# Lower parts of 16 weight tiles by an adding DMA, three pairs of part buffers and two raw slots, in a hybrid attention and DeltaNet layer

## The chip, the cores and the metric

The kernel runs on one core of a Trainium2 chip. The metric is the device time of one execution in microseconds (us), the median of several runs. The engines are named as in the profile: PE is TensorE's matmul and PEld its weight load, DVE is VectorE, ACT is ScalarE, POOL is GpSimd, and SP is SyncE, which here only issues transfers. An engine works through its queue in order.

## What is computed

One layer of a diffusion backbone on 512 latent tokens and 256 context tokens of width 1024, all in float32. Cut to what matters here:

```
h  = rms_norm(x)*(1+sc1)+sh1 ;  hc = the same for the context      # modulation: silu(c) @ w_ada
aq, ak, av, dq, dk, dv, dz, da, db, ga, gd = split(h @ w_in)       # context: hc @ w_in
y_attn = windowed attention (8 query heads, 2 key heads, window 128, context keys, sink)
o_dl   = gated DeltaNet, both directions, chunks of 64, started from the context's states
y   = sigmoid(ga)*(y_attn @ w_br_attn) + sigmoid(gd)*(norm(o_dl)*silu(dz) @ w_br_dn)
x   = x + gt1*(y @ w_out)
out = x + gt2*(square(relu(modulated_norm(x) @ w_mlp1)) @ w_mlp2)
```

## The kernel before

**Products in three parts.** A float32 operand is split into an upper part, rounded to the matmul's short float32 format (`fp32r`), and a lower part, what the rounding left. A product is then three matmuls, added up in PSUM: upper weight with upper input, upper weight with lower input, lower weight with upper input (`mm3`, L302 to L304; the same in L981 for the gate tiles and L1027 for the attention branch's projection). The lower part of a weight tile is so needed by the third matmul of a tile.

**Weight tiles.** A tile is 128 output columns of a matrix, 128 x 8 x 128 elements (512 KB; 256 KB for the branch projections). `wload` (L246) brings one in: SP loads it into a raw slot (`wr`, `NWR` = 4 slots, L248), ScalarE copies it, rounded, into the upper part (`wh`, L253), and VectorE subtracts that from the raw tile into the lower part (`wl`, L254). There are `NWS` = 2 pairs of `wh` and `wl`; a few calls give buffers of their own instead. A raw slot is free after the subtraction, a pair after the tile's last matmul.

**Which tiles go through it, and in which order.** Three early tiles in the prologue, with buffers of their own (L257 to L263); 60 tiles from the list `wq` (L363 to L366), in order: two key tiles of the DeltaNet (numbers 0 and 1), the attention's key tile (2), its four query tiles (3 to 6), its value tile (7), the DeltaNet's four value tiles (8 to 11) and four query tiles (12 to 15), three gate tiles (16 to 18), the attention branch's projection (19 to 26), 17 more gate tiles (27 to 43), the DeltaNet branch's projection (44 to 51), and the output projection (52 to 59). Then the MLP: tiles of `w_mlp1` with buffers of their own and 32 tiles of `w_mlp2`. A tile from the list is taken by `wnext` (L370), which hands out the tile that was prepared last time and calls `wload` for the next one, so one tile is prepared ahead:

```python
    wq = [lambda a=a: wload(*a) for a in wq]
    wn = [wq.pop(0)()]
    def wnext():
        w = wn.pop()
        if wq:
            wn.append(wq.pop(0)())
        return w
```

**Stages.** The prologue computes the modulation of the first norm (loads of `w_ada`, L213) and the modulated inputs, and multiplies the three early tiles along. Then the order of the code is woven: `weave` takes turns between generators of steps. The attention's key and query tiles are woven with the DeltaNet's decay matrices (`mats`, with L751 to L777 on VectorE); the rest of them, the value tile, the DeltaNet's value tiles and the first scores with the inversion of the chunks' triangular matrices (`invert`, L810 and L811, many small VectorE operations); the DeltaNet's query tiles and three gate tiles with the attention's units (`scores`: L507 to L536; `outputs`: transposes L566, splits L190 and L191, products L555 and L556, L587). After that come the context's scan beside the branch projection and gate tiles, the latent scan beside gate tiles, the DeltaNet branch's projection, the output projection and the MLP, which multiplies by seven products instead of eight in most of it (`Pair`, L1430).

**The other modulation weights.** `late_mod` (L1041) computes the other four modulation vectors on VectorE from 32 loads of `wada2`, 16 of them beside the latent scan, the rest around the output projection and the first MLP tiles. Each load takes a raw slot of the same tag `wr` (L1044), and the product is written to a piece of the arena (L1046 and L1047).

**Memory and order.** Most buffers come from an arena of 167 units of 1 KB per partition, handed out round robin (`alloc`). The order on each engine's queue follows the code, except that the framework's planner lets an instruction pass one that it expects to be blocked; on SP about 60 of the 205 loads stand elsewhere than in the code.

Of the kernel before, what the change touches and what calls it, by code (L numbers as in the profile page):

```python
# [8 lines left out]
F32 = mybir.dt.float32  # L9
F32R = mybir.dt.float32r  # L10
BF16 = mybir.dt.bfloat16
AF = mybir.ActivationFunctionType
ALU = mybir.AluOpType
# [1 line left out]
PSUM = bass.MemoryType.PSUM  # L15

NU = 167
NWR, NWS = 4, 2
FILL = 144, 28, 36, (8, 7, 3)
INV = 2, 12, 18, 0  # L20
QTS = 7, 5, 4, 7, 3, 6, 10, 7
# [13 lines left out]
P = 128  # L35
D = 1024
KT = D // P
# [65 lines left out]
def tile_layer(ctx: ExitStack, tc: tile.TileContext, I: dict, out: bass.AP, dbg=None):  # L103
    nc = tc.nc
    V, A, G, PE = nc.vector, nc.scalar, nc.gpsimd, nc.tensor
# [4 lines left out]
    wp = ctx.enter_context(tc.tile_pool(name="wp", bufs=1))  # L110
# [6 lines left out]
    def nm(s):  # L117
        uid[0] += 1
        return f"{s}_{uid[0]}"
# [8 lines left out]
    alloc, bank = mem.get, lambda n=1: banks.get(n * 512)  # L128
# [10 lines left out]
    r32 = lambda ap: ap.bitcast(F32R)  # L139
# [103 lines left out]
        V.tensor_scalar(modS[:, kt, :], mp[:, 1, :], bada[:, kt:kt + 1], None, op0=ALU.add)  # L243
        mp_.free()

    def wload(src, n=KT, bufs=None):  # L246
        raw = wp.tile([P, KT, P], F32, tag="wr", bufs=NWR, name=nm("wr"))[:, :n]
        nc.sync.dma_start(out=raw, in_=src)  # L248
        if bufs:
            hi, lo = (b.ap.rearrange("p (k c) -> p k c", k=KT) for b in bufs)  # L250
        else:
            hi, lo = (wp.tile([P, KT, P], F32, tag=t, bufs=NWS, name=nm(t))[:, :n] for t in ("wh", "wl"))
        A.activation(r32(hi), raw, AF.Copy)  # L253
        V.tensor_tensor(r32(lo), raw, hi, op=ALU.subtract)  # L254
        return r32(hi), r32(lo)

    early, EARLY = [], {T_AB: 0, T_DK: 0, T_DK + 1: 0}  # L257
# [2 lines left out]
    def load_early():  # L260
        bb = alloc(1024), alloc(1024)
        ebufs.extend(bb)
        early.append((wload(I["win"][list(EARLY)[len(early)]], bufs=bb), bank(2)))  # L263
# [10 lines left out]
    for src, nt, n, r in ((xs_, 4, SEQ, rx), (cs_, 2, CTX, rc)):  # L274
# [9 lines left out]
        w = 512  # L284
# [32 lines left out]
    for kt in range(KT):  # L317
        t = alloc(768)
# [38 lines left out]
    for n in range(2):  # L357
# [5 lines left out]
    wq = [(I["win"][t], KT) for t in (T_DK + 2, T_DK + 3, T_AK, *range(T_AQ, T_AQ + 4), T_AV, *range(T_DV, T_DV + 4),  # L363
                                      *range(T_DQ, T_DQ + 4), *(t + i for t, i in gates[:ND1]))]
    wq += [(I["wbr"][0, ct], 4) for ct in range(8)] + [(I["win"][t + i], KT) for t, i in gates[ND1:]]
    wq += [(I["wbr"][1, ct], 4) for ct in range(8)] + [(I["wout"][ct], KT) for ct in range(8)]  # L366
    wq = [lambda a=a: wload(*a) for a in wq]
    wn = [wq.pop(0)()]

    def wnext():  # L370
        w = wn.pop()
        if wq:
            wn.append(wq.pop(0)())
        return w

    def in_tile_steps(ti, with_ctx):

        for (_, e), t in zip(early, EARLY):
            if t == ti:
                return e  # L380
        w = wnext()
        acc = bank(2 if with_ctx else 1)
        for k in range(KT):
            mm3(acc[:, :512], w, hx[k:k + 1], start=(k == 0), stop=(k == KT - 1), ks=[k])
            if with_ctx:
                mm3(acc[:, 512:768], w, hc[k:k + 1], start=(k == 0), stop=(k == KT - 1), ks=[k])
            if k < KT - 1:
                yield
        return acc
# [258 lines left out]
    t, t2 = alloc(TOK), alloc(TOK)  # L648
# [325 lines left out]
    def gate_tiles(todo):  # L974

        for kind, i in todo:
            w = wnext()
            acc = bank()
            for k in range(KT):
                for p, (x, y) in enumerate(((0, 0), (0, 1), (1, 0))):  # L980
                    PE.matmul(acc.ap, w[x][:, k, :], hx[k][y], start=(k == p == 0), stop=(k == KT - 1 and p == 2))  # L981
                    yield
            if kind == T_GA:
                g = alloc(SEQ)
                act(g.ap, acc.ap, AF.Tanh, scale=0.5)
                V.scalar_tensor_tensor(gat[i].ap, g.ap, 1.0, gat[i].ap, op0=ALU.add, op1=ALU.mult)
                g.free()
            else:
                t = alloc(SEQ, True)
                if kind == T_GD:  # L990
                    act(t.ap, acc.ap, AF.Tanh, scale=0.5)
                else:
                    silu2(t.ap, acc.ap)
                (gdt if kind == T_GD else szt).append(t)
            acc.free()
# [23 lines left out]
    def br_a():  # L1019

        for ct in range(8):
            gat.append(alloc(SEQ, True))
            w = wnext()
            pa = bank()
            for j in range(4):
                for p, (x, y) in enumerate(((0, 0), (0, 1), (1, 0))):
                    PE.matmul(pa.ap, w[x][:, j, :], r32(Q[y][:, :, j, :]), start=(j == p == 0), stop=(j == 3 and p == 2))  # L1027
                    yield
            A.activation(gat[ct].ap, pa.ap, AF.Copy)
            pa.free()  # L1030
        for b in Qb:
            b.free()
# [6 lines left out]
    modT = const.tile([P, 4, 8], F32, name="modT")  # L1039

    def late_mod(grp):  # L1041

        for j in range(8):
            wa = wp.tile([P, KT, P], F32, tag="wr", bufs=NWR, name=nm("wa")).rearrange("p k c -> p (k c)")  # L1044
            nc.sync.dma_start(out=wa, in_=I["wada2"][grp, j])
            t = alloc(1024)  # L1046
            V.scalar_tensor_tensor(t.ap, wa, 0.5, scr.ap, op0=ALU.mult, op1=ALU.mult, accum_out=modT[:, grp, j:j + 1])  # L1047
            t.free()
            if j == 7:
                V.tensor_tensor(modT[:, grp], modT[:, grp], bada[:, 16 + 8 * grp:24 + 8 * grp], op=ALU.add)  # L1050
            yield

    late = (x for grp in range(4) for x in late_mod(grp))
    late_n = [0]

# [129 lines left out]
    scr = alloc(1024, True)  # L1185
# [22 lines left out]
    for g in range(2):  # L1208
# [12 lines left out]
        for a in range(2):  # L1221
            lo, hi = quad(a, 0), quad(a, 1)
# [36 lines left out]
    for qq in range(2):  # L1259
# [3 lines left out]
        for a in range(2):  # L1263
            n = 2 * qq + a
            t = alloc(512)
            ct = lambda ap: ap.rearrange("p (c t) -> p c t", t=CH)
            V.scalar_tensor_tensor(ct(t.ap), pt.ap.rearrange("p (c a t) -> p c a t", a=2, t=CH)[:, :, a], gdnh, ct(szt[n].ap),
                                   op0=ALU.mult, op1=ALU.mult)
# [12 lines left out]
    for ct in range(8):  # L1281
        w = wnext()
# [32 lines left out]
    for ct in range(8 - NHALF):  # L1315
        w = wnext()
# [35 lines left out]
    def load_first():  # L1352
        for i in range(NHALF):
            bufs = [alloc(1024), alloc(1024)]
            first.append([bufs, wload(I["wm1"][i], bufs=bufs)])
# [152 lines left out]
    for hf in range(4):  # L1508
        act_, xs = [], []
        for f in range(0 if hf else FT):  # L1510
            if first:
                bufs, _, acc = first.pop(0)
            else:
                bufs = [alloc(1024), alloc(1024)]
                w = wload(I["wm1"][f], bufs=bufs)
# [161 lines left out]
```

## Time and profile before

| | |
|---|---|
| median of 3 runs | 927.6 us (925.4 to 929.88) |
| the profiled execution | 928.46 us, of which the span of instructions 926.7 us |
| PE busy | 897.7 us, 97% of the span |
| PEld busy | 748.8 us, 81% |
| DVE busy | 665.5 us, 72% |
| ACT busy | 482.4 us, 52% |
| POOL busy | 12.1 us, 1% |
| HBM read | 95.46 MB; DMA 107 GB/s in the mean |
| granted TensorE clock | 0.998 |

The profile is of one execution. Ends of matmuls are modelled, so a PE that is busy is not a PE at its best rate; the matmuls of a tile follow each other every 0.23 us, although each is shown for longer. A row of a group gives engine, operation, output and inputs, shapes and count, then busy time and the mean duration of one in ns, then the engine's idle time ahead of the group and what ended it. The chain is the work that ended last, followed back from the end. Times of rows are from the start of the span.

### The profile page before, as it was taken

The numbers are of one execution on the slowest core, as the hardware profiler recorded it, in microseconds if no ns is written. First come the engines' busy times: TensorE is split into PE (matmuls) and PEld (weight loads), VectorE is DVE, ScalarE is ACT, GpSimd is POOL, SyncE is SP. The second block draws the span as 40 slices with busy tenths as digits, with TensorE's granted clock in tenths as the row PEclk, the third lists the DMA queues.
The fourth block names the chain that finished last, engine by engine and source line by source line (L and its number), as shares of the span: only waits on it lengthen the run. The fifth ranks groups of instructions, "written<-read, shape, count | busy, mean of one in ns | idle before, by whom it ended". The sixth has DMA issues, their size and how long they took to land.

```text
span 926.7 us, 19276 instructions
## 1 busy us (share of the span) xinstructions
PE 897.7 (97%) x8228; PEld 748.8 (81%) x8228; DVE 665.5 (72%) x1116; ACT 482.4 (52%) x857; POOL 12.1 (1%) x26
## 2 busy tenths in 40 slices
PE   8999999989999999999999999999999999999998
PEld 6688677867777787878888888987898899889976
DVE  4666799996877997367866978995587377538632
ACT  5467654357567787475554434563355145425420
POOL 0000000000000002000000000000000000000000
PEclk9999999999999999999999999999999999999999
DMA  9911112110000132324524575543313341232021
GB/s 362 366 47 47 48 48 69 47 46 24 22 15 23 58 115 72 115 93 140 182 71 148 184 252 190 179 140 113 137 47 109 103 152 43 94 129 99 2 91 45
DMA packets 29605, 98.79 MB, mean 107 GB/s; under 512 B 3664, under 2 KB 4176, under 8 KB 29520
## 3 DMA queue, kind: packets, MB, share of 16 engines
q1 hardware_dynamic: 29520, 97.57, 30.8%
q8 instruction: 64, 1.05, 0.5%
q14 instruction: 21, 0.17, 0.1%
HBM read 95.46 MB, written 2.10 MB: 105 GB/s over the span
## 4 chain that ended last, share of the span: by engine, by line
PE 64%; DVE 19%; ACT 7%; DMA 6%; issue 3%; SPq 0%; DVEq 0%; ACTq 0%
PE banks L1430 11%; PE banks L302 10%; PE banks L303 10%; PE banks L304 10%; PE banks L981 9%; DVE wl L254 3%; DVE m L191 2%; DMA m<-in_wm 2%; PE banks L1027 2%; PE banks L1093 2%; DMA wa<-in_wada 2%; ACT m L154 1%; DVE m L811 1%; PE banks L566 1%; DVE m L810 1%
## 5 line engine op out<-in xcount | busy, mean ns | idle before, releaser
L304 PE MATMUL banks<-m,wl 128*128 128x512 f32 (+1 forms) x568 | 210.6, 373 | 3.5 <-DVE wl L254 3.5
L302 PE MATMUL banks<-m,wh 128*128 128x512 f32 (+1 forms) x568 | 213.0, 376 | 0.6 <-ACT wh L253 0.2
L303 PE MATMUL banks<-m,wh 128*128 128x512 f32 (+1 forms) x568 | 210.3, 370 | 0.0
L253 ACT ACTIVATE wh<-wr 128x1024 fp32r<-128x1024 f32 (+1 forms) x92 | 90.4, 984 | 131.7 <-PE banks L303 104.5
L1430 PE MATMUL banks<-m,m 128*128 128x256 f32 x1008 | 125.7, 286 | 3.3 <-DMA m<-in_wm 2.0
L1430 PEld LDWEIGHTS banks<-m,m 128*128 128x128 f32 x1008 | 123.8, 194 | 5.5 <-DMA m<-in_wm 2.2
L254 DVE TENSOR_TENSOR wl<-wr,wh 128x1024 fp32r<-128x1024 f32 (+1 forms) x92 | 103.9, 1129 | 33.5 <-ACT wh L253 31.1
L304 PEld LDWEIGHTS banks<-m,wl 128*128 128x128 f32 x568 | 106.5, 188 | 23.3 <-DVE wl L254 5.4
L302 PEld LDWEIGHTS banks<-m,wh 128*128 128x128 f32 x568 | 107.0, 188 | 20.0 <-ACT wh L253 1.3
L190 ACT ACTIVATE m<-m 128x512 fp32r<-128x512 f32 (+2 forms) x118 | 82.3, 720 | 77.8 <-DVE m L1288 12.6
L303 PEld LDWEIGHTS banks<-m,wh 128*128 128x128 f32 x568 | 107.0, 188 | 17.7 <-DVE m L191 0.3
L191 DVE TENSOR_TENSOR m<-m,m 128x512 fp32r<-128x512 f32 (+2 forms) x118 | 92.5, 806 | 21.9 <-ACT m L190 17.1
L981 PE MATMUL banks<-m,wh 128*128 128x512 f32 x320 | 104.0, 399 | 1.3 <-ACT m L154 1.1
L1557 DVE SCALAR_TENSOR_TENSOR m<-banks,modT,m 128x512 f32<-128x512 f32 x32 | 24.0, 750 | 80.3 <-PE banks L304 80.3
L981 PEld LDWEIGHTS banks<-m,wh 128*128 128x128 f32 x320 | 59.3, 188 | 13.6 <-ACT m L154 1.3
L981 PE MATMUL banks<-m,wl 128*128 128x512 f32 x160 | 65.2, 408 | 0.0
L302 PE MATMUL banks<-m,m 128*128 128x256 f32 (+1 forms) x136 | 44.7, 342 | 2.0 <-ACT m L308 1.2
L1047 DVE SCALAR_TENSOR_TENSOR m<-wa,m 128x1024 f32<-128x1024 f32 x32 | 39.0, 1220 | 9.9 <-DMA wa<-in_wada 9.7
L303 PE MATMUL banks<-m,m 128*128 128x256 f32 (+1 forms) x136 | 45.4, 341 | 0.0
L304 PE MATMUL banks<-m,m 128*128 128x256 f32 (+1 forms) x136 | 44.5, 337 | 0.1
L154 ACT ACTIVATE m<-banks,st 128x512 f32<-128x512 f32 (+1 forms) x32 | 23.5, 738 | 25.7 <-DVE st L523 25.5
L981 PEld LDWEIGHTS banks<-m,wl 128*128 128x128 f32 x160 | 30.0, 188 | 6.5
(254 smaller groups left out, 1352.7 us busy)
## 6 DMA issues: line engine op xcount, KB each, us to landing
wr<-in_wm SPq DMA_DIRECT2D x40, 512.0 KB, 3.9
wr<-in_win SPq DMA_DIRECT2D x39, 512.0 KB, 3.4
wa<-in_wada SPq DMA_DIRECT2D x32, 512.0 KB, 3.6
m<-in_wm SPq DMA_DIRECT2D x24, 512.0 KB, 3.3
m<-in_wada SPq DMA_DIRECT2D x16, 512.0 KB, 9.9
m<-in_xT SPq DMA_DIRECT2D x8, 512.0 KB, 5.1
wr<-in_wbr SPq DMA_DIRECT2D x16, 256.0 KB, 2.6
wr<-in_wout SPq DMA_DIRECT2D x8, 512.0 KB, 4.3
```

Source lines behind the costliest of these rows:

```text
L154: r = A.activation(out_, in_, func, **kw)
L190: A.activation(r32(hi), src, AF.Copy)
L191: (eng or V).tensor_tensor(r32(lo), src, hi, op=ALU.subtract)
L253: A.activation(r32(hi), raw, AF.Copy)
L254: V.tensor_tensor(r32(lo), raw, hi, op=ALU.subtract)
L302: PE.matmul(acc, w[0][:, k, :], xhi, start=(start and i == 0), stop=False)
L303: PE.matmul(acc, w[0][:, k, :], xlo, start=False, stop=False)
L304: PE.matmul(acc, w[1][:, k, :], xhi, start=False, stop=(stop and i == n - 1))
L981: PE.matmul(acc.ap, w[x][:, k, :], hx[k][y], start=(k == p == 0), stop=(k == KT - 1 and p == 2))
L1047: V.scalar_tensor_tensor(t.ap, wa, 0.5, scr.ap, op0=ALU.mult, op1=ALU.mult, accum_out=modT[:, grp, j:j + 1])
L1430: PE.matmul(dst, r32(self.w[w][i][:, k * P:(k + 1) * P]), xs7[x][k][j], start=(n == 0), stop=(n == 11))
L1557: V.scalar_tensor_tensor(xn_[ct], accs[ct].ap, modT[:, 3, ct:ct + 1], xn_[ct], op0=ALU.mult, op1=ALU.add)
```

## The change

For tiles 3 to 18 of the list, the lower part is no longer made by VectorE. ScalarE copies the upper part a second time, with a scale of -1, into the lower part's buffer, and POOL issues a transfer that reads the same weights from HBM again and adds them to what lies there: weight minus upper part. The raw slot is then needed by the upper part's copy only. All tiles of the list are prepared two ahead instead of one. There are three pairs of part buffers instead of two and two raw slots instead of four, which is the same memory. The loads of `late_mod` no longer use raw slots: each goes to the piece of the arena that held the product, and the product is written over it.

```diff
-NWR, NWS = 4, 2
+NWR, NWS = 2, 3
+WAHEAD = 2
+LODMA = 3, 19
...
-    def wload(src, n=KT, bufs=None):
+    def wload(src, n=KT, bufs=None, late=False):
+
         raw = wp.tile([P, KT, P], F32, tag="wr", bufs=NWR, name=nm("wr"))[:, :n]
         nc.sync.dma_start(out=raw, in_=src)
...
         A.activation(r32(hi), raw, AF.Copy)
-        V.tensor_tensor(r32(lo), raw, hi, op=ALU.subtract)
+        if late:
+            A.activation(r32(lo), hi, AF.Copy, scale=-1.0)
+            G.dma_start(out=r32(lo), in_=src, accum_op=ALU.add)
+        else:
+            V.tensor_tensor(r32(lo), raw, hi, op=ALU.subtract)
         return r32(hi), r32(lo)
...
-    wq = [lambda a=a: wload(*a) for a in wq]
-    wn = [wq.pop(0)()]
+    wq = [lambda a=a, i=i: wload(*a, late=LODMA[0] <= i < LODMA[1]) for i, a in enumerate(wq)]
+    wn = [wq.pop(0)() for _ in range(WAHEAD)]
 
     def wnext():
-        w = wn.pop()
+        w = wn.pop(0)
         if wq:
             wn.append(wq.pop(0)())
         return w
...
         for j in range(8):
-            wa = wp.tile([P, KT, P], F32, tag="wr", bufs=NWR, name=nm("wa")).rearrange("p k c -> p (k c)")
-            nc.sync.dma_start(out=wa, in_=I["wada2"][grp, j])
-            t = alloc(1024)
-            V.scalar_tensor_tensor(t.ap, wa, 0.5, scr.ap, op0=ALU.mult, op1=ALU.mult, accum_out=modT[:, grp, j:j + 1])
-            t.free()
+            wa = alloc(1024)
+            nc.sync.dma_start(out=wa.ap, in_=I["wada2"][grp, j])
+            V.scalar_tensor_tensor(wa.ap, wa.ap, 0.5, scr.ap, op0=ALU.mult, op1=ALU.mult, accum_out=modT[:, grp, j:j + 1])
+            wa.free()
```

## The prediction

> **What bounds the kernel now.** I read the page's busy line first, then the busy tenths by slice (23.2 us each), then the shares of the chain that ended last.
>
> ```profile
> PE 897.7 (97%) x8228; PEld 748.8 (81%) x8228; DVE 665.5 (72%) x1116; ACT 482.4 (52%) x857; POOL 12.1 (1%) x26
> PE   8999999989999999999999999999999999999998
> DVE  4666799996877997367866978995587377538632
> ACT  5467654357567787475554434563355145425420
> DMA  9911112110000132324524575543313341232021
> PE 64%; DVE 19%; ACT 7%; DMA 6%; issue 3%; SPq 0%; DVEq 0%; ACTq 0%
> ```
>
> TensorE looks busy everywhere, yet the chain gives VectorE 19% of the span, and the slices show where: VectorE stands at 9 tenths from slice 5 to slice 8, while ScalarE stands at 3 to 5 and the DMA engines at 1 to 2. That is the attention input, in which 16 weight tiles are consumed that the change treats differently. So I asked for the two stretches around the attention, for the group of the lower-part subtractions in the first, and for the chain there (start, duration, what).
>
> ```profile
> 96.00:206.00 110.00, 103.67 (x1245) 81.55 (x1244) 103.74 (x188) 54.41 (x95) 2.07 (x4) 1.00 0.16 54
> 206.00:304.00 98.00, 91.57 (x654) 72.86 (x652) 75.42 (x128) 65.76 (x122) 0.00 (x0) 1.00 0.07 20
> L254 DVE TENSOR_TENSOR wl<-wr,wh 128x1024 fp32r<-128x1024 f32 x10 | 12.2, 1224 | 0.0
> 99.78 1.14 DVE wl L254
> 194.43 1.13 DVE wl L254
> ```
>
> The columns of the first two rows are the stretch, then the busy time of PE, PEld, DVE, ACT and POOL, granted clock, DMA share and GB/s. From 96 to 206 us VectorE is busy 103.74 of 110.00 us: it sets the pace. Ten of the 16 subtractions lie there, all ten on the chain; the last two rows are the first and the last, each worth 1.14 us of the chain. From 206 to 304 us (attention proper, a chain of scores, maximum, exponentials, transposes) no engine is full: DVE 75.42 and ACT 65.76 of 98.00 us. What TensorE itself lost shows in its weight loads' waits, for 96 to 206 us (first three rows) and for 206 to 304 us (total us, times, longest):
>
> ```profile
> PEld banks L756 <- DVE m L755: 2.3, 3, 1.3
> PEld banks L737 <- DVE m L769: 2.1, 2, 1.7
> PEld banks L304 <- DVE wl L254: 1.6, 1, 1.6
> PEld banks L556 <- DVE m L191: 2.6, 5, 0.9
> PEld banks L566 <- DVE m L581: 1.9, 2, 1.6
> PEld banks L841 <- ACT m L833: 1.8, 1, 1.8
> PEld banks L981 <- ACT m L154: 1.3, 1, 1.3
> ```
>
> In the first stretch TensorE waits 2.3 + 2.1 + 1.6 = 6.0 us for VectorE, and 110.00 - 103.67 = 6.3 us without work at all. This is what a lighter VectorE can win there before TensorE is the bound. In the second it waits 2.6 + 1.9 = 4.5 us for VectorE and 1.8 + 1.3 = 3.1 us for ScalarE.
>
> **The change part by part.** The durations:
>
> ```profile
> L254 DVE TENSOR_TENSOR wl<-wr,wh 128x1024 fp32r<-128x1024 f32 x76 | 92.9, 1222 | 28.0 <-ACT wh L253 25.6
> L253 ACT ACTIVATE wh<-wr 128x1024 fp32r<-128x1024 f32 x76 | 80.4, 1059 | 120.9 <-PE banks L303 104.2 <-DMA wr<-in_wm 6.8 <-PE banks L981 5.1
> wr<-in_win SPq DMA_DIRECT2D x39, 512.0 KB, 3.4
> m<-in_wada SPq DMA_DIRECT2D x16, 512.0 KB, 9.9
> ```
>
> *Removed:* 16 VectorE subtractions, 16 x 1.22 = 19.6 us of busy time, or 16 x 1.14 = 18.2 us of pace. In the first stretch 10 x 1.14 = 11.4 us leave a path that VectorE sets, but TensorE follows only until its own waits are gone. Bounds: 0 (TensorE's waits stay, for other instructions) and -11.4. I take **-6.0**, the waits on VectorE above. In the second stretch VectorE loses about five (5.7 us of pace) against 4.5 us of waits on it; this goes together with the next part.
>
> *Added on ScalarE:* 16 copies with scale -1, at the 1.06 us of the upper part's copy of the same shape: 17.0 us. In the first stretch they lie beside 110.00 - 54.41 = 55.6 us of idle ScalarE. Queued behind each is the next ScalarE work, the exponentials and attention splits, and VectorE and TensorE wait for those. In the second stretch the bounds are -4.5 (VectorE's waits all go) and +5.3 (five copies of 1.06 all on the path); I take **-1.0**, since waits on VectorE (4.5) outweigh those on ScalarE (3.1) by 1.4.
>
> *Added on POOL and the DMA engines:* 16 adding transfers of 512 KB. POOL is busy 2.07 us in the first stretch (four memsets) and not at all in the second, so issuing hides; behind a waiting issue stand only those memsets, which the joining of the inverse's halves needs late. No row shows a transfer that adds. The nearest are a plain one, 3.4 us to landing, and the 9.9 us of loads behind a full queue. It must also read what it adds to, so I bound it by 3.4 us and by twice 9.9 = 19.8, and take twice 3.4 = 6.8, as the DMA engines are 0.16 and 0.07 busy here. Is there cover? Upper parts are copied once per tile, two tiles ahead after the change, when the third tile back has left its buffer. Today's copies, every second one of the tightest row of tiles:
>
> ```profile
> 135.11 1.05 ACT L253 ACTIVATE wh<-wr 128x1024 fp32r<-128x1024 f32 x1
> 152.12 1.06 ACT L253 ACTIVATE wh<-wr 128x1024 fp32r<-128x1024 f32 x1 [0.70 <-PE banks L303]
> 170.84 1.05 ACT L253 ACTIVATE wh<-wr 128x1024 fp32r<-128x1024 f32 x1
> 188.82 1.06 ACT L253 ACTIVATE wh<-wr 128x1024 fp32r<-128x1024 f32 x1
> ```
>
> Two tiles last 17.0, 18.7 and 18.0 us. After two ScalarE copies (2.1 us) 14.9 us are left for a transfer of 6.8. It costs **0**; without that cover, the excess over 14.9 us.
>
> *Moved: three pairs of part buffers, two tiles ahead.* Today a lower part can come so late that TensorE waits; the 1.6 us above is one case and is counted. In the branch and output projections (480 to 565 us) there is another:
>
> ```profile
> PEld banks L304 <- DVE wl L254: 2.2, 3, 1.3
> 538.06 3.99 DMA wa<-in_wada
> SPq L1045 <- DVE wl L254: 55.2, 13, 11.2
> ```
>
> A third pair lets VectorE run a tile further ahead, so these 2.2 us can go: bounds 0 and -2.2. The modulation weights also leave the raw slots for the arena. Today their issue waits 55.2 us in total for a subtraction that frees a slot, and such loads stand on the chain (the second row is one of 3.99 us); from the arena they can be issued earlier. Both point one way: I take **-2.2**.
>
> *Two raw slots instead of four.* First place, the prologue, whose loads run at the DMA engines' limit (slices 0 and 1 at 9 tenths):
>
> ```profile
> 13.21 0.33 SPq L248 DMA_DIRECT2D wr<-in_win  x1
> 14.41 13.72 SPq L213 DMA_DIRECT2D m<-in_wada  x10
> 19.21 1.22 DVE L254 TENSOR_TENSOR m<-wr,m 128x1024 fp32r<-128x1024 f32 x1
> 28.52 1.04 ACT L253 ACTIVATE m<-wr 128x1024 fp32r<-128x1024 f32 x1
> ```
>
> The third early weight is issued at 13.21. With two slots it needs the slot of the first, free at 19.21 + 1.22 = 20.43, so 7.2 us later. If the planner lets the modulation loads pass (it orders SP's queue by readiness), the load lands at about 20.4 + 9.9 = 30.3 instead of before the copy at 28.52: +1.8. If SP stays blocked, up to +7.2. I take **+1.8**. Second place, the DeltaNet branch projection, with its short tiles:
>
> ```profile
> 500.00:524.00 24.00, 24.00 (x108) 19.81 (x106) 17.86 (x28) 11.55 (x18) 0.00 (x0) 1.00 0.55 186
> 502.34 0.23 PE banks L303
> wr<-in_wbr SPq DMA_DIRECT2D x16, 256.0 KB, 2.6
> L253 ACT ACTIVATE wh<-wr 128x512 fp32r<-128x512 f32 x16 | 10.0, 627 | 10.9 <-PE banks L981 8.3 <-PE banks L1027 2.3 <-PE banks L303 0.3
> L254 DVE TENSOR_TENSOR wl<-wr,wh 128x512 fp32r<-128x512 f32 x16 | 11.0, 686 | 5.5 <-ACT wh L253 5.5
> ```
>
> TensorE has no gap here; a tile is 12 matmuls of 0.23 = 2.8 us. A raw slot cycles in 2.6 + 0.63 + 0.69 = 3.9 us for two tiles of 5.5, which leaves 1.6 us for queueing; four residual loads of 512 KB pass through as well. Bounds 0 and +5 (about one transfer and a copy late); I take **+0.5**. In the MLP a tile is twice as long with the same two slots: 0.
>
> *Sum:* -6.0 - 1.0 + 0 - 2.2 + 1.8 + 0.5 = -6.9. The profiled execution took 928.46 us (span 926.7), 0.9 above the median of 927.6, so 921.6 on its own time and 920.7 on the median: **921 us**.
>
> The Trainium skill has a rule that speaks against the change: "SBUF — State Buffer", Who interferes with whom, says that a transfer issued from GpSimd has its descriptors built through a port pair shared with VectorE, and starves while VectorE runs copies, casts or tensor_scalar in a two-port mode, though not under tensor_tensor. By that exception the sum stays; were every VectorE instruction to block, the transfers would be late as in the third rival. The groups that I saw on VectorE there are tensor_tensor, reductions and transposes; no run here yet shows a transfer issued from POOL.
>
> **The rivals.**
> *All of the relief arrives.* VectorE's path shortens by 11.4 in the first stretch, and its 4.5 us of waits go in the second: 928.5 - 11.4 - 4.5 - 2.2 + 2.3 = 912.7 on the profiled execution's time, **912 us** on the median. For it: all ten subtractions are on the chain. Against: TensorE has only 6.3 us without work.
> *Another engine takes the place.* ScalarE's copies, put between a finished product and the next step, delay what VectorE gets, and the 7.0 us of relief go: 928.5 - 2.2 + 2.3 = 928.6, with half of the relief 925.1; **927 us**. For it: the waits on ScalarE after 206 us. Against: its 55.6 idle us.
> *The lower parts come too late (the other side).* Place: TensorE's first matmul with the lower part, tiles between 120 and 206 us. It decides from 14.9 us per transfer. At 19.8 us (or if POOL's issue is held up as long) a tile needs (2.1 + 19.8)/2 = 11.0 us against today's (188.82 - 135.11)/6 = 9.0, so 2.0 us on each of eight tiles: +16, and the relief of 6.0 is not felt: 921 + 16 + 6 = 943, less what slack at either end absorbs: about **938 us**. For it: no transfer of the kind is in the trace. Against: the nearest row says 3.4.
> *Two raw slots bind.* SP blocked for 7.2 us in the prologue and +5 in the branch projection, instead of 2.3: 921 + 9.9 = **931 us**. Against: the planner's freedom on SP, and a slot cycle shorter than two tiles.
> That the change doesn't do what it says (lower parts still on VectorE) the diff excludes.
>
> **How the numbers follow.** Chances: forecast 0.46 (own range 913 to 926), all relief 0.12, another engine 0.20, late lower parts 0.14, raw slots 0.08. A difference of 0.5%, 4.6 us, is about what a measurement of this kernel can tell from no change: 923.0 to 932.2. Faster: 0.36 of the forecast's share, 0.12, and 0.02 of the third case: 0.50. Same: 0.10 of the forecast, 0.16, 0.02 of the slots' case: 0.28. Slower: the rest, 0.22. The range reaches below the all-relief case and up to the late transfers: 908 to 938.
>
> **What would show it.** Right: VectorE's busy time from 96 to 206 us falls by about 12 us and the stretch shortens by some 6; the two ScalarE copies stand side by side; transfers on a POOL queue land in 5 to 10 us; no TensorE wait for that queue. Wrong: weight loads of L304 released by a DMA into the lower part; ScalarE's waits in TensorE's list above 5 us; the first matmul after the prologue later by more than 2 us; waits for raw weights from 500 to 524 us.

## The result, and the profile after

The changed kernel takes **919.7 us** (median of 5 runs, 918.87 to 921.45) against 927.25 us (5 runs, 925.4 to 929.88) of the kernel before: ratio 0.9921, 95% interval 0.9898 to 0.9943. The profiled execution took 919.03 us, its span 917.3. The prediction was 921.0. The number is right; most of its terms are not.

The page after, its busy line, the shares of its chain, and two rows of its transfers (the last number is us from issue to landing):

```profile
PE 892.9 (97%) x8228; PEld 748.7 (82%) x8228; DVE 648.8 (71%) x1100; ACT 497.5 (54%) x873; POOL 26.0 (3%) x42
PE 81%; DVE 8%; ACT 7%; issue 2%; DMA 2%; SPq 0%; ACTq 0%; DVEq 0%
wl<-in_win POOLq DMA_DIRECT2D x16, 512.0 KB, 5.5
m<-in_wada SPq DMA_DIRECT2D x48, 512.0 KB, 5.0
```

VectorE's share of the chain fell from 19% to 8% and TensorE's rose from 64% to 81%. The adding transfer lands 5.5 us after its issue, near the 6.8 that were estimated. The same two stretches around the attention as in the prediction, and three short ones (stretch, busy time of PE, PEld, DVE, ACT and POOL, granted clock, DMA share, GB/s), after:

```profile
24.00:28.00 4.00, 3.42 (x22) 1.54 (x22) 3.95 (x8) 1.75 (x3) 0.00 (x0) 0.76 1.01 398
28.00:32.00 4.00, 4.00 (x27) 3.20 (x19) 1.99 (x7) 2.45 (x4) 0.00 (x0) 0.81 1.02 419
96.00:206.00 110.00, 103.32 (x1216) 82.31 (x1206) 94.71 (x178) 63.95 (x105) 10.69 (x14) 0.98 0.46 102
145.00:150.00 5.00, 4.60 (x14) 3.24 (x15) 4.90 (x12) 3.29 (x5) 0.86 (x1) 0.66 0.23 21
206.00:304.00 98.00, 93.69 (x760) 74.52 (x749) 71.52 (x126) 70.15 (x128) 3.46 (x4) 1.00 0.21 44
```

The short ones before:

```profile
24.00:28.00 4.00, 3.44 (x24) 1.62 (x25) 3.98 (x8) 1.92 (x4) 0.00 (x0) 1.00 1.04 424
28.00:32.00 4.00, 4.00 (x30) 3.11 (x29) 3.10 (x8) 2.80 (x5) 0.00 (x0) 1.00 1.02 416
145.00:150.00 5.00, 5.00 (x31) 4.39 (x30) 4.91 (x11) 1.08 (x2) 0.00 (x0) 1.00 0.31 105
```

From 96 to 206 us VectorE's busy time fell by 9.0 us (103.74 to 94.71), yet TensorE works no longer in the stretch than before (103.32 against 103.67). What its weight loads mainly wait for there now (total us, times, longest):

```profile
PEld banks L414 <- ACT m L411: 4.7, 5, 2.4
PEld banks L744 <- issue: 3.9, 5, 2.2
PEld banks L573 <- ACT m L156: 1.7, 2, 1.4
PEld banks L744 <- DVE m L784: 0.9, 2, 0.5
PEld banks L744 <- DVE m L783: 0.8, 1, 0.8
```

VectorE is named for 1.7 us instead of 6.0; ScalarE for 6.4, where its rows before came to 3.8 (L411 is the square in the attention's norm of queries and keys). The waits changed their name more than their sum.

To see where the time came from, the next table sets the starts of the same work in each profiled execution against the kernel before, in us (minus is earlier). The columns are the last matmul of list tiles 0, 12, 18 and 57 (before: 70.0, 203.5, 301.2 and 553.9 us), the first output of the MLP's second quarter (713.7) and the last output (922.9). The lower rows are the experiments of the next section. Each row is one execution. "Clock" gives where its granted clock fell to half for 3.4 us (us from the start; before: 860), which costs a row up to 1.7 us.

| | tile 0 | tile 12 | tile 18 | tile 57 | 2nd quarter | last | clock |
|---|---|---|---|---|---|---|---|
| the change | +1.1 | +1.7 | -0.6 | -0.8 | -5.0 | -9.5 | 26, 146 |
| without adding transfers | +1.5 | +2.4 | +2.7 | +2.5 | -1.4 | -4.6 | 25, 155 |
| arena loads alone | -0.1 | 0.0 | +0.3 | -0.1 | -0.3 | -2.8 | none |
| third pair, one ahead, no adding | +1.2 | +1.1 | +1.1 | +1.0 | -3.2 | -6.4 | 25, 209 |
| the change, one ahead | +1.3 | +1.5 | -0.8 | -0.9 | -5.1 | -10.6 | 25, 117 |
| no lower work at all | +0.4 | +0.7 | -2.1 | -1.4 | -5.6 | -10.6 | 144 |
| negation on VectorE | +0.6 | -0.6 | -0.9 | -1.0 | -5.3 | -6.3 | 250, 854 |
| "list with two pairs" | +1.6 | +1.6 | 0.0 | -0.1 | -4.4 | -8.9 | 26, 129 |
| two raw slots alone | +1.5 | +1.5 | +1.3 | +1.1 | +4.9 | +2.7 | 26, 593 (twice as long) |
| early raw weights in the pairs | -0.4 | 0.0 | -2.2 | -2.5 | -1.5 | -5.9 | 115, 569 |

The last column flatters most of them: from 780 us on, the profiled execution before had one wait of 2.0 us for an MLP load, which is 0.6 us or less in all rows but the second, the fourth and the negation on VectorE, and a drop of the granted clock, which of the others only the negation on VectorE had there:

```profile
PE banks L1430 <- DMA m<-in_wm: 2.0, 1, 2.0
```

```profile
860.00:890.00 30.00, 29.98 (x192) 27.51 (x191) 16.18 (x25) 13.47 (x16) 0.00 (x0) 0.95 0.01 2
```

So the column of the second quarter is the one to read.

Through the attention, where the prediction saw 7.0 of its 9.2 us of gains, the change moved the end of tile 18 by 0.6 us (from tile 0 on by 1.7 us, with a drop of the clock on the way). More than 4 us came between tile 57 and the MLP's second quarter, where the prediction saw nothing.

### The profile page after: what moved, and what is told of

Same layout as the page of the kernel before. It is cut to its first block, busy times and chain, and to the rows that moved or that the text cites. A ratio compares the mean times of both kernels' runs of the same rounds, so it can differ in the third digit from the quotient of the medians.

```text
span 917.3 us, 19321 instructions
## 1 busy us (share of the span) xinstructions
PE 892.9 (97%) x8228; PEld 748.7 (82%) x8228; DVE 648.8 (71%) x1100; ACT 497.5 (54%) x873; POOL 26.0 (3%) x42
## 4 chain that ended last, share of the span: by engine, by line
PE 81%; DVE 8%; ACT 7%; issue 2%; DMA 2%; SPq 0%; ACTq 0%; DVEq 0%
PE banks L309 14%; PE banks L310 14%; PE banks L311 14%; PE banks L988 11%; PE banks L1436 11%; PE banks L1034 2%; PE banks L1099 2%; ACT m L156 2%; PE banks L1111 1%; DMA m<-in_wm 1%; PE banks L1130 1%; PE banks L573 1%; DVE m L193 1%; PE banks L636 1%; PE banks L744 1%
## 5 line engine op out<-in xcount | busy, mean ns | idle before, releaser
L1436 PE MATMUL banks<-m,m 128*128 128x256 f32 x1008 | 123.6, 284 | 1.8 <-DVE m L193 1.0
L1436 PEld LDWEIGHTS banks<-m,m 128*128 128x128 f32 x1008 | 121.9, 192 | 3.6 <-DVE m L193 1.7
L192 ACT ACTIVATE m<-m 128x512 fp32r<-128x512 f32 (+2 forms) x118 | 82.5, 720 | 73.2 <-PE banks L1436 13.4
L261 DVE TENSOR_TENSOR wl<-wr,wh 128x1024 fp32r<-128x1024 f32 (+1 forms) x76 | 84.2, 1109 | 26.2 <-ACT wh L256 24.0
L1053 DVE SCALAR_TENSOR_TENSOR m<-m,m 128x1024 f32<-128x1024 f32 x32 | 38.9, 1219 | 12.3 <-DMA m<-in_wada 12.2
```

Source lines behind the costliest of these rows:

```text
L192: A.activation(r32(hi), src, AF.Copy)
L1053: V.scalar_tensor_tensor(wa.ap, wa.ap, 0.5, scr.ap, op0=ALU.mult, op1=ALU.mult, accum_out=modT[:, grp, j:j + 1])
L1436: PE.matmul(dst, r32(self.w[w][i][:, k * P:(k + 1) * P]), xs7[x][k][j], start=(n == 0), stop=(n == 11))
```

## The experiments

The first experiments take the change apart, the later ones test the reasons. Each ratio is to the kernel before, timed beside it; differences between experiments are given in us of the 927 us.

**Without the adding transfers.**

```diff
-LODMA = 3, 19
+LODMA = 0, 0
```

> The changed kernel with an empty list of adding transfers (LODMA = 0, 0): all lower parts are subtracted on VectorE again; three pairs of part buffers, two raw slots, two tiles ahead and the modulation weights in the arena stay. Theory of the buffers (the profile of after shows the attention stretch no shorter, and 7 of the 9 us won lie behind 500 us): 916 to 922 us. Theory of the prediction (the adding transfers win 6.0 us from 96 to 206 us and 1.0 behind it, the rest nets to 0): 926 to 928 us.

Measured: 923.49 us, ratio 0.9957 (0.9942 to 0.9973). It lies between the two: the buffers alone win 4 us, and the adding transfers another 3.3 us (0.9921 against 0.9957). By the table their share is there at tile 18: +2.7 without them, -0.6 with them, 3.3 us. Little of it comes before tile 12: from tile 0 to there, each with one drop of the clock, the run without them lost 0.9 us and the change 0.6.

**The adding transfers alone**, on the kernel before, with its four raw slots, two pairs and one tile ahead.

```diff
 NWR, NWS = 4, 2
+WAHEAD = 1
+LODMA = 3, 19
...
```

> The kernel before with the adding transfers for tiles 3 to 18 and nothing else: four raw slots, two pairs, one tile ahead, modulation weights in raw slots. Theory of the buffers: 925 to 930 us, as the negated copies on ScalarE eat what VectorE wins; with one tile ahead there are about 9 us a tile, less 2.1 for the two copies, against 5.5 to landing, so no long wait for lower parts. Theory of the prediction: 921 to 923 us.

Measured: 925.35 us, ratio 0.9978 (0.9963 to 0.9994): 2.0 us, not the 7.0 of the prediction's two terms. Here TensorE does wait for the new transfer, from 90 to 304 us:

```profile
PEld banks L311 <- DMA wl<-in_win: 3.0, 2, 2.1
```

No such row stands among the waits of the changed kernel from 96 to 304 us. With two pairs the transfer's 5.5 us are not always covered; with three they are.

**The modulation weights' loads into the arena alone.**

```diff
-            wa = wp.tile([P, KT, P], F32, tag="wr", bufs=NWR, name=nm("wa")).rearrange("p k c -> p (k c)")
+            wa = alloc(1024)
...
```

> The kernel before with the 32 modulation weights of late_mod loaded into the arena instead of raw slots, nothing else. If the loads that waited for a slot (55.2 us of SP's queue, transfers on the chain from 530 to 561 us) cost the path: 922 to 925 us. If the third pair of part buffers is what wins: 926 to 928 us.

Measured: 927.27 us, ratio 0.9997 (0.9981 to 1.0013): nothing. The 55.2 us that these loads' issue waited cost nobody anything.

**The third pair without the rest**: three pairs, two raw slots, arena loads; one ahead, no adding.

```diff
-WAHEAD = 2
-LODMA = 3, 19
+WAHEAD = 1
+LODMA = 0, 0
```

> Two raw slots and three pairs, the modulation weights in the arena, one tile ahead, no adding transfers. The MLP's tiles don't come from the list, so there three pairs act in the same way with one ahead as with two. If the gain is the MLP's and the projections' third pair: 917 to 923 us, within 3 us of the kernel with two ahead. If two ahead is what wins: 924 to 928 us.

Measured: 921.04 us, ratio 0.9930 (0.9913 to 0.9946). This is most of the whole change, from the part that the prediction gave -2.2 for the pair against +2.3 for the raw slots.

**The change one tile ahead.**

```diff
-WAHEAD = 2
+WAHEAD = 1
```

> The changed kernel with the list loaded one tile ahead instead of two; the adding transfers and the third pair stay. Theory that two ahead costs (without the adding transfers the third pair alone gave 921.0 and two ahead on top 923.5, +2.45): it costs here too, 917 to 918.5 us. Theory that two ahead is what the adding transfers need, since the lower part comes a copy, an issue of 0.9 us and a transfer of 5.5 us after the upper one: without it TensorE waits for that transfer, 921 to 925 us.

Measured: 918.11 us, ratio 0.9905 (0.9878 to 0.9932). The adding transfers don't need the second tile ahead, since three pairs give the lead already. Whether two ahead costs something in the changed kernel isn't told apart: the intervals of 0.9905 and 0.9921 overlap. Without adding transfers it cost 2.5 us (0.9930 against 0.9957, whose intervals just touch); why is not shown. The 2.3 us between this run and the one without adding transfers (0.9905 and 0.9930) lie within overlapping intervals too; only with two ahead do the adding transfers stand clear of noise (3.3 us).

**No lower part made at all** in the 16 tiles, by anyone.

```diff
-            A.activation(r32(lo), hi, AF.Copy, scale=-1.0)
-            G.dma_start(out=r32(lo), in_=src, accum_op=ALU.add)
+            lo = hi
```

> The changed kernel, but in the 16 tiles no lower part is made at all: neither negated copy on ScalarE nor adding transfer; the third matmul of each group reads the upper part again, so the output leaves the weights' lower parts of these tiles wrong. Theory that ScalarE has taken VectorE's place (16 negated copies of 1.06 us stand ahead of the squares and copies for which TensorE now waits 2.4 and 2.8 us): 914 to 917 us. Theory that neither engine sets the end of this stretch any more, and the rest of the gap is the clock and the prologue: 919 to 920 us.

The third matmul then reads the upper part again, so the output lacks the lower parts of these weights.

Measured: 918.94 us, ratio 0.9915 (0.9892 to 0.9937), the changed kernel's time. This is the ceiling: with neither subtraction nor copy nor transfer the attention gives no more than the change already takes, as far as ratios of 0.9915 and 0.9921 can tell. The same stretches:

```profile
96.00:206.00 110.00, 103.85 (x1243) 82.56 (x1242) 95.47 (x179) 55.51 (x97) 2.07 (x4) 0.98 0.16 54
206.00:304.00 98.00, 93.22 (x658) 74.25 (x657) 72.14 (x129) 66.50 (x126) 0.00 (x0) 1.00 0.07 23
```

and TensorE's first waits from 96 to 206 us:

```profile
PEld banks L413 <- ACT m L410: 3.9, 5, 2.6
PEld banks L743 <- issue: 2.9, 5, 1.5
PEld banks L743 <- DVE m L775: 2.3, 2, 1.5
```

ScalarE is back at 55.51 us busy, and TensorE still waits 3.9 us for its squares (L410 here is L411 after). So the negated copies do not cause that wait. More than half of it is one place, and ScalarE's order makes it. In the changed kernel the square there stands behind the splits of the norm before it (L192), and those wait for VectorE's last product of that norm (L425):

```profile
143.44 1.28 ACT L192 ACTIVATE m<-m 64x512 fp32r<-64x512 f32 x2 [1.67 <-DVE m L425]
144.75 0.60 ACT L411 ACTIVATE m<-banks 128x512 f32<-128x512 f32 x1
```

Without lower work the order is the same (141.50 and 142.81 us), and TensorE waits 2.6 us there. In the kernel before (140.81 and 144.82 us) and with the negation on VectorE the square goes first, and all the waits for squares come to 1.3 and 1.7 us:

```profile
142.19 0.58 ACT L411 ACTIVATE m<-banks 128x512 f32<-128x512 f32 x1
145.29 1.29 ACT L192 ACTIVATE m<-m 64x512 fp32r<-64x512 f32 x2 [1.95 <-DVE m L425]
```

No run puts the square first where VectorE has no lower parts to make, so what this order costs is not shown.

**The negation on VectorE** instead of ScalarE.

```diff
-            A.activation(r32(lo), hi, AF.Copy, scale=-1.0)
+            V.tensor_scalar(r32(lo), hi, -1.0, None, op0=ALU.mult)
```

> The changed kernel with the negated copy made by VectorE from the upper part (one source, instead of the subtraction of two); ScalarE is left with the upper part alone. ScalarE theory: 917 to 919 us if VectorE's copy of one source is well shorter than the subtraction's 1.2 us, about 920 to 922 us if it is as long. VectorE theory (the change wins only what it takes off VectorE): back to the kernel without adding transfers, 922 to 924 us. By the Trainium skill, page SBUF — State Buffer, section Who interferes with whom, a VectorE copy in a two-port mode starves transfers whose descriptors GpSimd writes: then the adding transfers land later than 5.5 us after their issue.

Measured: 918.82 us, ratio 0.9915 (0.9893 to 0.9937). That lies in the range of the ScalarE theory, but the run before it had already taken ScalarE's copies away and won nothing. VectorE has 7 us more to do than in the changed kernel (101.64 against 94.71 us busy from 96 to 206 us), ScalarE 8 us less, and the time is the same: it follows neither engine. From tile 0 to tile 12, where no drop of the clock struck this run, it gained about 1.1 us. The copies and their transfers from 96 to 304 us:

```profile
L258 DVE TENSOR_SCALAR wl<-wh 128x1024 fp32r<-128x1024 f32 x14 | 9.6, 686 | 1.6 <-ACT wh L256 1.6
wl<-in_win POOLq DMA_DIRECT2D x14, 512.0 KB, 5.7
96.00:206.00 110.00, 103.36 (x1248) 82.16 (x1248) 101.64 (x191) 56.33 (x99) 11.02 (x14) 1.00 0.44 102
```

VectorE's copy of one source takes 0.69 us, where its subtraction of two took 1.22. The transfers land after 5.7 us instead of 5.5. The Trainium skill's rule that the prediction weighed ("SBUF — State Buffer", Who interferes with whom) names VectorE's tensor_scalar, where it runs in a two-port mode, as one that starves transfers issued from GpSimd. Here there is 0.2 us of it at most; 14 such copies in 208 us are too few to say more.

**The early tiles' raw weights in memory of their own.** The branch for tiles with buffers of their own also takes the first tiles of `w_mlp1`.

```diff
+        own = alloc(1024, True) if bufs else None
+        if bufs:
+            raw = own.ap.rearrange("p (k c) -> p k c", k=KT)
+        else:
+            raw = wp.tile([P, KT, P], F32, tag="wr", bufs=NWR, name=nm("wr"))[:, :n]
-        raw = wp.tile([P, KT, P], F32, tag="wr", bufs=NWR, name=nm("wr"))[:, :n]
...
+        if own:
+            own.free()
```

> The changed kernel one tile ahead, and the raw weights of the three early tiles in memory of their own, so that the two raw slots no longer hold back the third early load in the prologue. Theory that this load costs the start 1.1 to 1.5 us (the end of the first tile after against before): 1 to 2 us under the run with one tile ahead, and the DMA moves 400 GB/s or more at 20 to 24 us. Theory that the start is hidden behind what TensorE computes from 30 to 96 us: the same as that run within 0.5 us.

Measured: 929.79 us, ratio 1.0023 (1.0006 to 1.0041), 11 us behind the run with one tile ahead. Its prologue, against which the theory was made, got worse:

```profile
20.00:24.00 4.00, 2.45 (x19) 1.28 (x15) 2.79 (x5) 2.01 (x5) 0.00 (x0) 0.93 0.74 304
24.00:28.00 4.00, 3.72 (x18) 2.18 (x17) 3.20 (x7) 2.57 (x4) 0.00 (x0) 0.50 0.00 0
```

From 24 to 28 us nothing is transferred at all. That the new buffers moved others in working memory, and with them the plan of the loads, is the likely reason, but not shown. The run says nothing on the raw slots' price.

**The list with two pairs, the MLP with three** was meant by this edit on the kernel with the third pair, one ahead and no adding:

```diff
             wn.append(wq.pop(0)())
+            if len(wq) % 2:
+                for t in ("wh", "wl"):
+                    G.memset(wp.tile([P, KT, P], F32, tag=t, bufs=NWS, name=nm("skip"))[:, 0, :4], 0.0)
```

> The third pair with one tile ahead and no adding transfers (921.0 us before), but the list of tiles left with two pairs: after every second tile of the list one pair is skipped (four columns written by GpSimd hold its place), so only the MLP has three. Theory of the prediction (the third pair earns in the list's short tiles at 480 to 565 us, nothing in the MLP): what it won is lost, 925 to 928 us, and TensorE again waits some 2 us for lower parts at 552 to 566 us. Theory that most of it is won in the MLP, whose first weights are then ready when the list ends: 921 to 923 us.

Measured: 920.42 us, ratio 0.9938 (0.9914 to 0.9962). It says nothing on either theory, since the edit did not do what it was to do: the next tile took the skipped slot, and the loads ran as far ahead as with three pairs (the first weights of the MLP are issued at 548.01 us here, at 549.09 with three pairs). It is the third pair once more, 0.9938 and 0.9930. As such it corrects the other run's row: from tile 12 to tile 18 it gains about 1.5 us, where the other gains nothing, but with a drop of the clock in that stretch:

```profile
209.00:213.00 4.00, 3.61 (x127) 3.42 (x126) 2.28 (x3) 2.94 (x5) 0.00 (x0) 0.57 0.16 30
```

**Two raw slots alone**, with two pairs, one ahead, arena loads, no adding.

```diff
-NWR, NWS = 2, 3
+NWR, NWS = 2, 2
-WAHEAD = 2
-LODMA = 3, 19
+WAHEAD = 1
+LODMA = 0, 0
```

> The kernel before with two raw slots instead of four, two pairs, one tile ahead, the modulation weights in working memory (with four raw slots that gave 927.3 us): nothing is won, only the raw slots are taken. Theory of the prediction (1.8 us in the prologue, 0.5 in the DeltaNet branch projection): 928.5 to 930.5 us. Theory that two raw slots cost nothing, because two pairs limit the loads anyway: 926 to 928 us. If it is faster than 926, the gain put down to the third pair came from the raw slots, through another order of the loads.

Measured: 931.16 us, ratio 1.0045 (1.0030 to 1.0060): 4.2 us slower than before, above both theories. The table shows where: +1.1 at tile 57, +4.9 in the MLP's second quarter. Between them TensorE waits for the lower part of a weight tile of the MLP, from 554 to 606 us:

```profile
PEld banks L311 <- DVE m L261: 4.2, 1, 4.2
```

and the stretches around it show a full VectorE ahead of the wait and a lower granted clock behind it, which takes another 0.23 x 15 = 3.4 us:

```profile
575.00:590.00 15.00, 15.00 (x124) 14.83 (x123) 15.00 (x35) 8.64 (x18) 0.00 (x0) 1.00 0.33 110
590.00:605.00 15.00, 11.28 (x39) 8.78 (x38) 10.60 (x15) 6.55 (x10) 0.00 (x0) 0.77 0.52 176
```

The loads at the end of the list (start, duration) say why. With two raw slots and two pairs:

```profile
549.19 0.33 SPq L251 DMA_DIRECT2D wr<-in_wout  x1
554.63 0.33 SPq L251 DMA_DIRECT2D wr<-in_wm  x1
```

With two raw slots and three pairs, one ahead, no adding (the first of three):

```profile
543.64 0.33 SPq L251 DMA_DIRECT2D wr<-in_wout  x1
549.09 6.90 SPq L251 DMA_DIRECT2D wr<-in_wm  x3
```

The MLP's first weights are issued 5.5 us earlier, a whole tile, and the wait of 4.2 us is not in that run. The only edit between the two runs is the third pair: 1.0045 to 0.9930, **10.7 us**. By the table 8.0 us of it come between tile 57 (+1.1 and +1.0) and the second quarter (+4.9 and -3.2). In the list, "list with two pairs", which is the third pair without a drop of the clock at 209 us, is 1.2 us earlier at tile 57 (-0.1). So the third pair does a little in the list and most of its work at the passage into the MLP.

The code says what is special there: the last three tiles of the list are held together, because each is used for two halves of the tokens. With two pairs the third of them finds no pair until one of the others is through; its upper part is copied 8.8 us later, and until its lower part is made too its raw weights keep one of the two raw slots. First with two pairs, then with three:

```profile
561.02 1.06 ACT L256 ACTIVATE wh<-wr 128x1024 fp32r<-128x1024 f32 x1 [1.16 <-issue]
552.18 1.06 ACT L256 ACTIVATE wh<-wr 128x1024 fp32r<-128x1024 f32 x1 [3.84 <-PE banks L310]
```

The kernel before, with four raw slots, copies this part at 561.48 us as well.

**The early raw weights in the lower parts' slots**, on the change one ahead; again the first tiles of `w_mlp1` go with them.

```diff
-        raw = wp.tile([P, KT, P], F32, tag="wr", bufs=NWR, name=nm("wr"))[:, :n]
+        tag, nb = ("wl", NWS) if bufs else ("wr", NWR)
+        raw = wp.tile([P, KT, P], F32, tag=tag, bufs=nb, name=nm("wr"))[:, :n]
```

> The changed kernel one tile ahead (918.1 us), with the raw weights of the three early tiles in the lower parts' three slots, which are free in the prologue; no working memory moves, unlike the run that put them there (929.8). Theory that the third early load, held back by two raw slots, costs 1.1 to 1.3 us at the end of the first tile: 916.5 to 917.5 us. Theory that the change of plan in the prologue costs more than the slot, as it did there by a gap of the DMA at 24 to 28 us: 920 us or more.

Measured: 923.99 us, ratio 0.9963 (0.9944 to 0.9981), 5.4 us behind the run without the edit. At tile 0 it stands at -0.4 instead of +1.3 (a drop of the clock in the other's prologue is part of that), and the lead stays up to tile 57 (-2.5 against -0.9). The loss comes behind it, because the MLP's raw weights now sit in slots of lower parts. What SP waits for from 545 to 650 us, and a weight load of TensorE from 561 to 650 us:

```profile
SPq L252 <- PE banks L312: 11.7, 3, 8.2
PEld banks L310 <- ACT m L316: 2.6, 3, 1.8
```

A raw load that must wait until TensorE has used a lower part comes late. So the edit helped the start and spoilt the passage into the MLP; for the early tiles alone it was not run.

**The adding transfer for 17 gate tiles more**, on the last run.

```diff
-late=LODMA[0] <= i < LODMA[1])
+late=3 <= i < 19 or 27 <= i < 44)
```

> The run with the early raw weights in the lower parts' slots, and the adding transfer for the 17 gate tiles behind the DeltaNet branch projection (340 to 500 us) as well. Theory that subtractions can be taken off VectorE with profit only where TensorE waits for VectorE through the attention: within 1 us of that run. Theory that they pay wherever the recurrences leave TensorE gaps (10 us of them at 395 to 480 us): 2 to 4 us under it. Theory that the adding transfer comes too late for a list one tile ahead: 2 us or more over it, and TensorE's waits name GpSimd's queue.

Measured: 932.37 us, ratio 1.0069 (1.0046 to 1.0092), 9.8 us behind the last run. None of the three theories: it loses, yet TensorE never waits for GpSimd's queue. What VectorE waits for from 410 to 505 us, first here, then in the last run:

```profile
DVE m L1054 <- DMA m<-in_wada: 20.3, 13, 2.5
```

```profile
DVE m L1054 <- DMA m<-in_wada: 7.7, 6, 2.8
```

And the transfers from 340 to 505 us, first here, then in the last run (a group's last number is us to landing):

```profile
DMA packets 7743, 27.68 MB, mean 168 GB/s; under 512 B 864, under 2 KB 864, under 8 KB 7716
m<-in_wada SPq DMA_DIRECT2D x20, 512.0 KB, 5.0
wl<-in_win POOLq DMA_DIRECT2D x16, 512.0 KB, 7.3
```

```profile
DMA packets 6498, 22.66 MB, mean 137 GB/s; under 512 B 715, under 2 KB 715, under 8 KB 6471
m<-in_wada SPq DMA_DIRECT2D x22, 512.0 KB, 4.1
```

The transfers move 137 GB/s in the last run and 168 here. The modulation weights land 0.9 us later, VectorE stands in order behind the products that wait for them, and the scan's steps stand behind VectorE. The chain of this run gives 54.2% of the time from 425 to 470 us to these loads. How much of this is the later landing is not shown: VectorE, without the subtractions, also comes to these products earlier, and so waits longer for the same load.

## Why the prediction was right or wrong

**The sum was right by errors that cancel, and so by luck.** Taken from ratios, along one path of runs: arena loads 0, two raw slots +4.2, third pair -10.7, adding transfers -2.3 (0.9930 to 0.9905) and second tile ahead +1.5 (0.9905 to 0.9921), neither told from 0 alone: -7.3. Predicted: adding transfers -7.0, pairs with arena loads and two ahead -2.2, raw slots +2.3: -6.9.

**"Removed, first stretch: -6.0"** failed. From tile 0 to tile 12 the change lost 0.6 us. A drop of the granted clock took at most 1.7 of that (0.34 of 5 us at 145 us), so the relief is worth 1.1 at the most; with no lower work at all 1.4 by the same reckoning (0.3 lost, one drop). Against the run without adding transfers, which also had a drop, it is 0.3, and the negation on VectorE, without one, gained 1.1. VectorE was said to set the pace there, but TensorE was as full (103.67 of 110.00 us against 103.74). The step took TensorE's waits with VectorE's name as what a lighter VectorE wins. But they were the last to end, not the only ones: the squares, the transposes' copies and the issue stood close behind. With VectorE lighter, ScalarE's order also changed so that one square waits behind work that itself waits for VectorE (2.4 of the 4.7 us that now go to the squares).

**"Second stretch: -1.0"** was mis-sized on the other side: from tile 12 to tile 18 the change won 2.3 us (+1.7 to -0.6) and no lower work at all 2.8. Without adding transfers this stretch lost 0.3 with two ahead, but with three pairs and one ahead it won about 1.5 ("list with two pairs"); so whether all of the 2.3 is VectorE's relief stays open. Of the waits on VectorE that the prediction listed, about half were won there (4.5 us) and at most a quarter in the first stretch (6.0 us): the fuller stretch gave less.

**The rival "another engine takes the place"** had the outcome of the first stretch and not its mechanism. TensorE does wait for ScalarE instead, 6.4 us, beyond the 5 us that the prediction set as its mark. But ScalarE's added copies are not the cause: without them the wait for the squares is 3.9, and with the negation moved to VectorE the time is the same.

**The adding transfer at 0** held: 5.5 us to landing, no wait for it in the changed kernel. The reason given, a lead of two tiles, was not the needed one; three pairs with one ahead serve as well. The rival of late lower parts had the right place only in the kernel with two pairs (3.0 us of waits).

**"Third pair, two ahead and arena loads: -2.2"** failed in place and size. The arena loads give 0. The third pair gives 10.7 us against two raw slots with two pairs, about 1.2 of it in the list. The 2.2 us of waits for lower parts at 480 to 565 us did go (TensorE has no gap left from 480 to 566 us), but they are the smaller part.

**"In the MLP a tile is twice as long with the same two slots: 0"** is the step that failed worst. It looked at the steady state of the MLP, where nothing changes, and not at the passage into it: there the last three tiles of the list need three pairs at once, the norm fills VectorE, and weights that come a tile later meet it. Two slots alone cost 3.8 us there (+1.1 to +4.9), the drop of the clock behind the wait included; the third pair takes that back and 4.2 more (+1.0 to -3.2).

**"Two raw slots, prologue: +1.8"** can't be read from the runs with a clock dip at 24 to 32 us, which alone moves tile 0 (+2.0 with four raw slots and such a dip, in the run of the adding transfers alone). Without a dip, two slots show +0.4 (no lower work) and +0.6 (negation on VectorE), four -0.1: some 0.6 us. The cause was seen rightly: DMA moves 320 GB/s at 20 to 24 us instead of 419. **"DeltaNet branch projection: +0.5"** is 0; TensorE has no gap from 480 to 520 us (40.00 us busy).

What the prediction gave as signs: VectorE's busy time fell by 9.0 instead of 12, and the stretch did not shorten by 6. That sign alone would have shown the first term wrong, whatever the total.

## What to carry to other kernels

Waits listed by releaser are not a sum to be won: when TensorE is busy for 94% of a stretch, the next waits stand right behind the ones removed. One run that leaves the work out altogether gives the ceiling, and should come first. The lead of a weight queue was worth most here where one stage hands over to the next, more tiles are held at once, and the engine that prepares weights has a burst of its own; so buffers are to be judged there too and not in the steady state alone. A transfer that replaces an engine's work is not free where that engine waits for other transfers beside it.

## What the runs showed of the hardware

**The granted clock falls in pieces of one size.** The two windows of the prologue after lose 0.24 x 4 + 0.19 x 4 = 1.7 us, the one at 145 us 0.34 x 5 = 1.7. Taken alone, the drop at 145 us is 3.41 us at half clock (second row); the first row is the 3.41 us ahead of it:

```profile
142.13:145.54 3.41, 1.46 (x9) 0.94 (x8) 3.21 (x10) 2.02 (x4) 0.00 (x0) 1.00 0.51 161
145.54:148.95 3.41, 3.41 (x8) 2.18 (x9) 3.31 (x10) 2.78 (x4) 0.86 (x1) 0.50 0.17 10
```

The Trainium skill, "TensorE: Matmul & The Clock Gate", Part 1, tells of a monitor with a free-running window of about 3.4 us, after which an idle TensorE goes to half its clock. An estimate from that figure is a loss of 1.7 us for one window, and the rows agree. The runs differ from the Trainium skill in what goes ahead: TensorE was not idle for a window, but busy for 1.46 of 3.41 us here and for 2.27 of 3.41 ahead of the drop at 26 us. It strikes a kernel whose TensorE is 97% busy, and not each time: the gaps of TensorE at 22.8 and 23.9 us (0.49 and 0.64 us) are the same before and after, and only the execution after lost its clock behind them. At 143 us a gap of 1.95 us went ahead of the drop after; before, one of 1.44 us at 142.8 went without. Each such drop is 0.2% of the span. It moves single profiles by as much as the effects that were looked for here.

**An adding transfer of 512 KB** takes 5.5 us from issue to landing, against 3.3 of a plain load of the same weights in the same kernel, and its issue keeps GpSimd for 0.86 us.

```profile
wr<-in_win SPq DMA_DIRECT2D x39, 512.0 KB, 3.3
L259 POOL DMA_DIRECT2D wl<-in_win x10 | 8.6, 862 | 103.5 <-ACT wl L258 103.5
```
